# All five instruction queues of a fp32r encoder trunk in an order given by a table, in place of the scheduler's order with hand exceptions

## The chip, the cores and the metric

One core of a Trainium2 chip runs the whole program. Its engines work side by side, each through its own queue of instructions in a fixed order: PE (matmuls; PEld is its weight load), ACT, DVE, POOL, and SP, which here only starts transfers. An instruction waits on semaphores for what others have to deliver, and all behind it on its queue wait too. The metric is the device time of one execution in microseconds (us).

## What is computed

A trunk of two encoder layers over 512 tokens of width 1024, all in float32. Layer 0 mixes tokens by neighbourhood attention on a grid 64 wide (16 heads of 64), layer 1 by multi-head latent attention (low-rank queries and keys, a rotary part, dense). Each layer:

```python
xn = rmsnorm(x, norm_g[i])
y = mixer(xn)            # na: q,k,v,z = xn@w_in ; (attention * silu(z)) @ w_out
h = x + y                # mla: c_q,c_kv,k_rope,z = xn@w_in ; q, kv from the low ranks
gate = sigmoid(rmsnorm(h, ple_norm[i]) @ ple_w_gate[i])
x = h + gate * (p[i] @ ple_w_proj[i])
...
return rmsnorm(x, final_norm)
```

## The kernel before

Every matrix product is made of three fp32r products: each operand is split into a rounded part "hi" and a rest "lo" (ACT makes hi by a copy, DVE or POOL the rest by a subtraction), and hi·hi + hi·lo + lo·hi are summed in PSUM, in matmuls of 128 x 512. PSUM tiles are named by their use: ps_mm, ps_S (scores), ps_T (transposes), ps_O (outputs).

The stages and their times in the run before:

- Start to 45 us: warm-up matmuls, the per-layer embedding of layer 0 (ple, L673, out to memory as pe), the gates z (z_phase) of layer 0 from the raw x, split xT.
- 45 to 105 us: values_seven (L267). The values x@w_v are made by seven products on quarters in place of eight. Its weights W7 and W5 are sums of two quarters: `load` (L273) loads one quarter through SP's queue, and then POOL's queue starts a transfer that accumulates the other into it (L276). W7's tile is later summed with raw pieces on DVE to serve products 6 and 4. `made` splits a piece into whi (ACT) and wlo (DVE). Products 1, 2, 7, 6, 5, 4, 3 follow on PE (L301), between them queries and keys of the first two head pairs (L413). after1, after7, after6 and after5 copy sums out of PSUM (s1, s17, s6) and add them to other banks, so that a product continues a bank which ACT and DVE have just read. All that ACT and DVE do here is written in the order in which it is issued: both are wrapped in InOrder, which adds a dependency of each instruction on the one before.
- 105 to 230 us: the heads of neighbourhood attention (na_head, L536): scores on PE (L558, L559), bias and maximum on DVE, exponential on ACT, scaling on POOL (L582), transposes on PE (L594, L596), split, output (L608). Projections of the next heads (L123) run in between, and POOL starts the accumulating transfers of the gate's weight sums (L730).
- 230 to 395 us: output projection, gate of layer 0 (gate_seven, also in seven products), the low-rank projections of layer 1, z.
- 395 to 560 us: the dense heads (mla_heads, L942). `score` (L1041), `turn` (L1058) and `output` (L1066) are put by hand into 70 steps: at step i the score of step i, the transposes of step i - 3, and outputs two heads back; the projections of the next pair are cut up and added to the steps by `pieces`. qe and qo get their rotary rows by transfers from rh and rl (L117).
- 560 us to the end: output projection, gate of layer 1, final norm, written out by halves of rows.

Order before: the program is traced once; a scheduler with a time model then gives every queue its order by the dependences between tiles. Where that was not wanted, an issue_after written in the code adds an order dependency: 25 places, some on a chain of instructions (PE's in values_seven, na_heads and mla_heads, ACT's and DVE's in values_seven), others on a single one (a load that has to come behind a certain copy, `gn` behind the last load). SP's transfers go through eight semaphores in turn, so that one waits until that of eight earlier has landed.

Of the kernel before, what the change touches and what calls it, by code (L numbers as in the profile page):

```python
# [40 lines left out]
class InOrder:  # L41
# [4 lines left out]
    def __getattr__(self, name):  # L46
        call = getattr(self.engine, name)

        def run(*args, **kw):
            with self.tc.issue_after(self.last.ins) if self.last is not None else nullcontext():  # L50
                self.last = call(*args, **kw)
            return self.last

        return run


class Trunk:
# [122 lines left out]
    def z_phase(self, wap, xT, js, after=None, R=None, ws=None, first=None):  # L180
# [5 lines left out]
        def finish(j, ps):  # L186
            z = zs[j] = self.zp.tile([P, S], F32, name="z", tag="z")
            with self.tc.issue_after(after) if after is not None else nullcontext():
                if R is None:
                    nc.scalar.activation(z, ps, AF.Silu)  # L190
                else:
                    nc.vector.tensor_tensor(out=z, in0=ps, in1=R, op=ALU.mult)
                    nc.scalar.activation(z, z, AF.Silu)
# [73 lines left out]
    def values_seven(self, pool, xT, xk, Q, pair, more):  # L267
# [23 lines left out]
        def product(p):  # L291
# [3 lines left out]
            for c, i in [(0, 0), (0, 1), (1, 0), (1, 1)] if p in (1, 2, 7) else [(0, 0), (1, 0), (0, 1), (1, 1)]:  # L295
# [3 lines left out]
                for j, (l, r) in enumerate(m):  # L299
                    with self.tc.issue_after(self.last_mm.ins):  # L300
                        self.last_mm = nc.tensor.matmul(ps, l, r, start=c == 0 and j == 0 and p in banks,  # L301
                                                        stop=c == 1 and j == 5 and p in (2, 3, 4),
                                                        skip_group_check=True)
# [102 lines left out]
    def na_heads(self, pool, xT, zs, Q, xk, weights, more):  # L406
# [3 lines left out]
        def product(out, w):  # L410
            for i, (l, r) in enumerate(self.terms(w, xT, range(KD))):
                with self.tc.issue_after(self.last_mm.ins):
                    self.last_mm = nc.tensor.matmul(out, l, r, start=i == 0, stop=i == 3 * KD - 1)  # L413
# [13 lines left out]
        def edges(q, last):  # L427
            s0 = []
            for s in q:
                e0 = pool.tile([P, P], F32R, name="s0", tag="s0", bufs=4)  # L430
                with self.tc.issue_after(last.ins):
                    self.act.activation(e0.rearrange("p (a b) -> p a b", a=2),
                                        win(s, 0, P, 0, [[448, 2], [1, 64]]).bitcast(F32), AF.Copy)
# [59 lines left out]
        def attend(j, also):  # L493
            sq, s0, dk, kl = A.pop(j)
            O = []
            for e in range(2):
# [3 lines left out]
                with self.tc.issue_after(self.last_norm.ins):  # L500
                    also(e)
# [34 lines left out]
    def na_head(self, pool, h, sq, s0, dk, kl, vh):  # L536
# [9 lines left out]
        for half in range(2):  # L546
# [25 lines left out]
            for i in range(2):  # L572
                qt = 2 * half + i
                e = ex[:, ecol(qt)]
                with self.tc.issue_after(self.hold):
                    self.last_exp = nc.scalar.activation(e, e, AF.Exp, scale=-1.0, bias=mx[:, qt:qt + 1],  # L576
                                                         accum_out=sm[:, qt:qt + 1])
# [44 lines left out]
    def out_proj(self, wap, oT, res, after, last_mm):  # L622
        nc = self.nc
        for n in range(2):
            ws = [self.load_w(wap[n, c], 1024, extra=n == 1 or c == 3, rest=nc.vector if self.wxn > 5 and c % 2 else None)
                  for c in range(4)]
            for u, t in enumerate(range(NT)):
# [4 lines left out]
                with self.tc.issue_after(last_mm):  # L632
# [842 lines left out]
```

## Time and profile before

| | us |
|---|---|
| median of 3 runs | 652.93 (652.9 to 653.29) |
| profiled execution | 653.56 |
| its span | 651.5 |
| busy: PE, PEld, DVE, ACT, POOL | 640.2, 541.9, 427.7, 453.4, 408.4 |

The span runs from the first to the last instruction that the trace has; about 2 us of the execution lie outside. Matmul ends are modelled, and matmuls overlap, so a time on PE is best counted from start to start. In rows of the trace the first number is the start, the second the time that the group covers; in brackets stands how long the engine was idle before it and what ended that.

### The profile page before, as it was taken

To read this page: it belongs to the slowest core of one execution; us is meant where nothing else is said; L and a number is where in the kernel's file an instruction comes from. 1 tells how busy PE (TensorE), PEld (TensorE's weight loads), DVE (VectorE), ACT (ScalarE), POOL (GpSimd) and SP (SyncE) were. 2 spreads that over 40 slices of the span, in tenths; PEclk is the share of its full clock that TensorE was granted. 3 is DMA by queue.
4 is the path that set the end of the run, shared out by engine and by line. 5 is a ranking of instruction groups with operands and counts; after the bars stand their busy time and mean duration, and the time that the engine had idled before them with its cause. 6 is when DMAs were issued, how large, how long until landed. Compare 5 with 4: busy or idle time off the path is not lost.

```text
span 651.5 us, 9980 instructions
## 1 busy us (share of the span) xinstructions
PE 640.2 (98%) x3299; PEld 541.9 (83%) x3299; DVE 427.7 (66%) x886; ACT 453.4 (70%) x903; POOL 408.4 (63%) x371
## 2 busy tenths in 40 slices
PE   9999999999999999999999999999999999999994
PEld 6888878888888888888999887888888888888884
DVE  6197987565665616569715514898988885474665
ACT  7575766887886733788644535897989897547855
POOL 0471006877978853797655516786969887437974
PEclk9999999999999999999999999999999999999997
DMA  9939725778958989446643245120112223683524
GB/s 326 355 124 306 217 66 179 263 205 217 229 209 217 239 178 342 147 154 188 224 140 102 78 109 156 32 75 24 49 50 66 65 84 112 229 292 126 193 65 162
DMA packets 46131, 107.41 MB, mean 165 GB/s; under 512 B 4736, under 2 KB 17792, under 8 KB 46080
## 3 DMA queue, kind: packets, MB, share of 16 engines
q1 hardware_dynamic: 34608, 87.12, 39.3%
q0 software_dynamic: 11040, 18.88, 13.6%
q10 hardware_dynamic: 432, 0.79, 0.3%
q8 instruction: 26, 0.43, 0.3%
q14 instruction: 25, 0.20, 0.1%
HBM read 95.23 MB, written 25.17 MB: 185 GB/s over the span
## 4 chain that ended last, share of the span: by engine, by line
PE 83%; POOL 1%; ACT 1%; DVE 0%; DMA 0%; issue 0%; POOLq 0%
PE ps_mm L123 27%; PE ps_S L123 10%; PE ps_mm L959 7%; PE ps_T L155 6%; PE ps_T L851 5%; PE ps_O L1071 5%; PE ps_mm L851 3%; PE ps_S L851 3%; PE ps_O L608 2%; PE ps_T L123 2%; PE ps_O L123 2%; PE ps_mm L909 2%; PE ps_T L301 2%; PE ps_T L596 2%; PE ps_S L909 1%; PE ps_S L559 1%
## 5 line engine op out<-in xcount | busy, mean ns | idle before, releaser
L101 POOL TENSOR_TENSOR wwlo<-wraw,wwhi 128x1024 fp32r<-128x1024 f32 (+5 forms) x68 | 122.3, 1810 | 93.5 <-ACT wwhi L100 41.9
L796 POOL TENSOR_TENSOR wlo<-wraw,whi 128x512 fp32r<-128x512 f32 x56 | 72.7, 1331 | 22.3 <-ACT whi L794 20.2
L1056 POOL TENSOR_TENSOR ex<-ex,rc 128x512 f32<-128x512 f32 x64 | 66.2, 1043 | 26.6 <-DVE rc L1055 22.5
L100 ACT ACTIVATE wwhi<-wraw 128x1024 fp32r<-128x1024 f32 (+5 forms) x71 | 55.1, 799 | 34.3 <-PE ps_mm L123 18.9
L1054 ACT ACTIVATE ex<-ps_S,mx 128x512 f32<-128x512 f32 x64 | 44.0, 687 | 12.6 <-DVE mx L1052 10.9
L1052 DVE TENSOR_REDUCE mx<-ps_S 128x1 f32<-128x512 f32 x64 | 43.7, 683 | 8.4 <-PE ps_S L123 7.7
L582 POOL TENSOR_TENSOR ex<-ex,rc 128x128 f32<-128x128 f32 (+1 forms) x64 | 37.5, 701 | 17.7 <-DVE rc L578 17.5
L112 DVE TENSOR_TENSOR pt_lo<-ps_T,pt_hi 128x512 fp32r<-128x512 f32 x64 | 43.1, 680 | 7.1 <-ACT pt_hi L110 6.7
L110 ACT ACTIVATE pt_hi<-ps_T 128x512 fp32r<-128x512 f32 x64 | 37.7, 594 | 3.4 <-PE ps_T L155 3.0
L155 PE MATMUL ps_T<-ident,ex 128*128 128x128 f32 x256 | 38.3, 272 | 0.0
L155 PEld LDWEIGHTS ps_T<-ident,ex 128*128 128x128 f32 x256 | 31.5, 140 | 7.5
L123 PE MATMUL ps_mm<-xh,wwhi 128*128 128x512 f32 x120 | 33.7, 404 | 0.0
L221 DVE TENSOR_TENSOR u<-ps_O,u 64x512 f32<-64x512 f32 x32 | 21.9, 685 | 17.7 <-ACT u L220 17.2
L576 ACT ACTIVATE ex<-ex,mx 128x128 f32<-128x128 f32 (+1 forms) x64 | 30.2, 473 | 4.2 <-DVE mx L565 4.1
L123 PE MATMUL ps_mm<-xl,wwhi 128*128 128x512 f32 x120 | 31.9, 395 | 0.0
L794 ACT ACTIVATE whi<-wraw 128x1024 fp32r<-128x1024 f32 x28 | 29.3, 1057 | 3.2 <-DMA wraw<-sum 2.4
L123 PE MATMUL ps_mm<-xh,wwlo 128*128 128x512 f32 x120 | 31.1, 394 | 0.0
L123 PE MATMUL ps_S<-ke,qe 96*128 96x512 f32 x96 | 28.9, 407 | 0.3 <-DMA qe<-rl 0.3
L123 PE MATMUL ps_S<-ko,qo 128*128 128x512 f32 x96 | 28.9, 409 | 0.0
L959 PE MATMUL ps_mm<-cT,wwhi 128*128 128x512 f32 x94 | 27.7, 393 | 0.0
L220 ACT ACTIVATE u<-ps_O 64x512 f32<-64x512 f32 x32 | 18.9, 591 | 12.0 <-PE ps_O L608 8.8
L225 POOL TENSOR_TENSOR u<-u,z 128x512 f32<-128x512 f32 x16 | 22.6, 1412 | 7.5 <-DVE u L221 7.5
(488 smaller groups left out, 1915.1 us busy)
## 6 DMA issues: line engine op xcount, KB each, us to landing
sum<-gate POOLq DMA_DIRECT2D x12, 1024.0 KB, 8.2
wraw<-na_qk SPq DMA_DIRECT2D x16, 512.0 KB, 4.9
wraw<-sum SPq DMA_DIRECT2D x16, 512.0 KB, 3.3
pe<-pe SPq DMA_DIRECT2D x31, 256.0 KB, 5.9
wraw<-gate SPq DMA_DIRECT2D x12, 512.0 KB, 3.3
wraw<-na_v SPq DMA_DIRECT2D x10, 512.0 KB, 3.4
sum<-sum POOLq DMA_DIRECT2D x4, 1024.0 KB, 11.1
wraw<-na_o SPq DMA_DIRECT2D x8, 512.0 KB, 4.8
```

The source lines that it names most:

```text
L100: nc.scalar.activation(hi[:, c], raw[:, c], AF.Copy)
L101: f = lambda e, c=c: e.tensor_tensor(out=lo[:, c], in0=raw[:, c], in1=hi[:, c].bitcast(F32), op=ALU.subtract)
L110: self.last_copy = self.act.activation(hi, src, AF.Copy, scale=scale)
L112: self.dve.tensor_tensor(out=lo, in0=src, in1=hi.bitcast(F32), op=ALU.subtract)
L123: last = self.last_mm = nc.tensor.matmul(out, l, r, start=i == 0, stop=i == n - 1)
L155: self.last_mm = self.nc.tensor.transpose(t[:, i * P:(i + 1) * P], b, self.ident)
L796: nc.gpsimd.tensor_tensor(out=lo[:, o], in0=raw[:, o], in1=hi[:, o].bitcast(F32), op=ALU.subtract)
L851: mm = nc.tensor.matmul(ps, l, r, start=j == 0 and p in banks, stop=j == 11 and p in (2, 3, 4), skip_group_check=True)
L959: self.last_mm = nc.tensor.matmul(PS[key], *terms[i], start=i == 0, stop=i == len(terms) - 1)
L1052: nc.vector.reduce_max(mx, sp, axis=AX.X, negate=True)
L1054: nc.scalar.activation(ex, sp, AF.Exp, bias=mx, accum_out=sm)
L1056: nc.gpsimd.tensor_tensor(out=ex, in0=ex, in1=rc.to_broadcast([P, S]), op=ALU.mult)
```

## The change

All issue_after's go, and with them the order written into InOrder. In their place a table, ORDER, has for each engine a list of runs of indices: its instructions, numbered as the program writes them, in the order in which they are now to stand. A function, called when the whole trunk is traced, adds an order dependency (no semaphore) of each instruction on the one ahead of it:

```python
ORDER = dict(
    PE=(
        "0-9 11 14-15 12 35 13 16 36 41 37 23-24 42 20 25-26 53-56 21-22 17-19 10 47 43 38 29-30 44 31-33 63-64 57 "
...
def in_order(tc):
    engines = dict(PE="PE", ACT="Activation", DVE="DVE", POOL="Pool", SP="SP")
    traced = [i for i in tc.nc.cur_bb.bb.instructions if "Boundary" not in type(i).__name__]
    behind = mybir.DependencyInfo(mybir.DependencyClass.NoSync, mybir.DependencyReason.DATA)
    for e, runs in ORDER.items():
        mine = [i for i in traced if i.engine == getattr(mybir.EngineType, engines[e])]
        order = []
        for run in runs.split():
            a, _, b = run.partition("-")
            order += mine[int(a):int(b or a) + 1]
        assert len(order) == len(mine) == len(set(i.name for i in order))
        for x, y in zip(order, order[1:]):
            tc.add_manual_dep(y, x.name, behind, reason="in_order")


def trunk_kernel(tc, a):
    with ExitStack() as ctx:
        Trunk(tc, ctx, a).run()
        in_order(tc)
```

The exceptions are taken out in this manner:

```diff
-            with self.tc.issue_after(self.last.ins) if self.last is not None else nullcontext():
-                self.last = call(*args, **kw)
+            self.last = call(*args, **kw)
...
-                    with self.tc.issue_after(self.last_mm.ins):
-                        self.last_mm = nc.tensor.matmul(ps, l, r, start=c == 0 and j == 0 and p in banks,
-                                                        stop=c == 1 and j == 5 and p in (2, 3, 4),
-                                                        skip_group_check=True)
+                    self.last_mm = nc.tensor.matmul(ps, l, r, start=c == 0 and j == 0 and p in banks,
+                                                    stop=c == 1 and j == 5 and p in (2, 3, 4),
+                                                    skip_group_check=True)
```

The instructions, their operands and their number are the same in both programs. The order differs all along: rows that stood together on PE are dealt out among others almost everywhere. Three places follow; the line numbers of the new program are a little smaller.

SP's queue where the weights of values_seven are loaded (W7, W5: the summed weights; wraw_637, 717, 719 and on from na_v: raw pieces of values; wraw_647 and 655: weights of the second head pair). Before:

```order
L252 DMA wraw_543<-na_v 128x1024
L275 DMA W7_519<-na_v 128x2x1024
L275 DMA W5_539<-na_v 128x2x1024
L252 DMA wraw_637<-na_v 128x1024
L457 DMA wraw_647<-na_qk 128x1024
L457 DMA wraw_655<-na_qk 128x1024
L252 DMA wraw_717<-na_v 128x1024
L252 DMA wraw_719<-na_v 128x1024
L252 DMA wraw_733<-na_v 128x1024
```

Now:

```order
L250 DMA wraw_543<-na_v 128x1024
L678 DMA pe03_93<-pe_299 128x512
L250 DMA wraw_637<-na_v 128x1024
L273 DMA W7_519<-na_v 128x2x1024
L452 DMA wraw_647<-na_qk 128x1024
L452 DMA wraw_655<-na_qk 128x1024
L250 DMA wraw_717<-na_v 128x1024
L250 DMA wraw_719<-na_v 128x1024
L273 DMA W5_539<-na_v 128x2x1024
L250 DMA wraw_733<-na_v 128x1024
```

W7's load stands behind one raw piece that it stood ahead of, and W5's behind five.

ACT's queue in the same stage, around the products 6 and 5 (whi_799 and 840 are W5's halves, whi_851 and 890 those of the weight of product 4, s17 and s6 the copies out of PSUM). Before:

```order
L51 ACTIVATE whi_799<-W5_539 128x1024
L51 ACTIVATE da_830<-ps_mm_738 64x512 x2
L51 ACTIVATE db_831<-ps_mm_738 64x512 x2
L51 ACTIVATE s0_836<-sa_787 128x128
L51 ACTIVATE s0_838<-sb_788 128x128
L51 ACTIVATE whi_840<-W5_539 128x1024
L51 ACTIVATE s17_846<-ps_T_804 128x512
L51 ACTIVATE s17_849<-ps_T_805 128x512
L51 ACTIVATE whi_851<-W7_519 128x1024
L51 ACTIVATE s6_884<-ps_T_858 128x512
L51 ACTIVATE s6_887<-ps_O_859 128x512
```

Now:

```order
L50 ACTIVATE whi_851<-W7_519 128x1024
L50 ACTIVATE sa_787<-ps_mm_737 64x512
L50 ACTIVATE sb_788<-ps_mm_737 64x512
L50 ACTIVATE whi_799<-W5_539 128x1024
L50 ACTIVATE whi_840<-W5_539 128x1024
L50 ACTIVATE da_830<-ps_mm_738 64x512 x2
L50 ACTIVATE s17_849<-ps_T_805 128x512
L50 ACTIVATE s17_846<-ps_T_804 128x512
L50 ACTIVATE db_831<-ps_mm_738 64x512
L50 ACTIVATE s6_884<-ps_T_858 128x512
L50 ACTIVATE s6_887<-ps_O_859 128x512
```

whi_851 stands ahead of both halves of W5, and both of these ahead of the copies.

PE's queue at the end of a dense head's transposes (ps_T_5731 is the last of the head whose output is ps_O_5795; ps_S are scores of the next, ps_mm_5747 its projection). Before:

```order
L155 MATMUL ps_T_5731<-ident_71,ex_5628 128x128 x4
L123 MATMUL ps_S_5738<-ke00_3473,qe00_3469 128x512
L123 MATMUL ps_S_5738<-ke01_3474,qe00_3469 128x512
L123 MATMUL ps_S_5738<-ke00_3473,qe01_3470 128x512
L959 MATMUL ps_mm_5747<-cT0_3467,wwhi_5406 128x512 x2
L959 MATMUL ps_mm_5747<-cT1_3468,wwhi_5406 128x512 x2
L155 MATMUL ps_T_5754<-ident_71,ex_5665 128x128 x4
L123 MATMUL ps_S_5764<-ko00_3475,qo00_3471 128x512
L123 MATMUL ps_S_5764<-ko01_3476,qo00_3471 128x512
L123 MATMUL ps_S_5764<-ko00_3475,qo01_3472 128x512
L959 MATMUL ps_mm_5747<-cT0_3467,wwlo_5407 128x512 x2
L155 MATMUL ps_T_5788<-ident_71,ex_5688 128x128 x4
```

Now:

```order
L154 MATMUL ps_T_5731<-ident_71,ex_5628 128x128 x3
L122 MATMUL ps_S_5738<-ke00_3473,qe01_3470 128x512
L154 MATMUL ps_T_5731<-ident_71,ex_5628 128x128
L122 MATMUL ps_S_5764<-ko00_3475,qo00_3471 128x512
L122 MATMUL ps_S_5764<-ko01_3476,qo00_3471 128x512
L122 MATMUL ps_S_5764<-ko00_3475,qo01_3472 128x512
L154 MATMUL ps_T_5754<-ident_71,ex_5665 128x128 x2
L1050 MATMUL ps_O_5795<-pt_hi_5648,vt_5149 128x512 x2
L154 MATMUL ps_T_5754<-ident_71,ex_5665 128x128 x2
L154 MATMUL ps_T_5788<-ident_71,ex_5688 128x128 x2
```

The output's first matmuls, which came behind two more sets of transposes and their scores, now follow after three score matmuls and two transposes.

More of the change, by code (lines that the diff above doesn't have):

```diff
@@ L187, in finish @@
             z = zs[j] = self.zp.tile([P, S], F32, name="z", tag="z")
[L188 to L193, printed above, removed]
+            if R is None:
+                nc.scalar.activation(z, ps, AF.Silu)
+            else:
+                nc.vector.tensor_tensor(out=z, in0=ps, in1=R, op=ALU.mult)
+                nc.scalar.activation(z, z, AF.Silu)
         if ws:
@@ L671, in ple @@
                         for i in (0, 1, 2, 6, 7, 8, 3, 4, 5, 9, 10, 11):
[L672 to L673 removed]
+                            last = nc.tensor.matmul(first[i // 6][0], *first[i // 6][1][i % 6], start=i % 6 == 0, stop=i % 6 == 5)
                 else:
@@ L907, in mla_c @@
                 for j, (l, r) in enumerate(m):
-                    with self.tc.issue_after(self.turned[t + 1].ins) if (part, j) == (0, 12) and t < 3 else nullcontext():
-                        mm = nc.tensor.matmul(ps[:, :wn], l, r, start=j == 0, stop=j == 23)
+                    mm = nc.tensor.matmul(ps[:, :wn], l, r, start=j == 0, stop=j == 23)
                 nc.scalar.activation(cs[t][:, w0:w0 + wn], ps[:, :wn], AF.Copy)
@@ L1145, in mla_heads @@
         rope(0, 0, 9)
[L1146 to L1147 removed]
+        late[0]()
         queries(0, 0, 9, "S")
@@ L1377, in run @@
                     last = self.mla_heads(hpool, x1T, cT, sets, oT)
+ORDER = dict(
+    PE=(
[100 rows of a table added]
+    ),
+    ACT=(
[26 rows of a table added]
+    ),
+    DVE=(
[28 rows of a table added]
+    ),
+    POOL=(
[12 rows of a table added]
+    ),
+    SP=(
[8 rows of a table added]
+    ),
+)
+def in_order(tc):
[11 more added lines that the diff above has]
+            tc.add_manual_dep(y, x.name, behind, reason="in_order")
 def trunk_kernel(tc, a):
```

65 lines of the change are left out of this document (21 added, 44 removed), and 173 rows, old and new, of tables (ACT, DVE, PE, POOL).

## The prediction

> **What bounds the kernel now.** I read the busy time by stage first, then the engine that is busiest there, then what makes it wait. By stage (columns: length, busy time and count of each engine, TensorE clock, DMA share, GB/s):
>
> ```profile
> core 0: us, PE busy (x) PEld busy (x) DVE busy (x) ACT busy (x) POOL busy (x), PEclk, DMA share, GB/s
> 0.00:5.26 5.26, 4.50 (x11) 1.46 (x11) 0.60 (x2) 2.43 (x3) 0.19 (x4) 1.00 0.67 209
> 45.00:105.00 60.00, 58.82 (x264) 48.66 (x263) 52.47 (x68) 35.54 (x51) 9.09 (x8) 1.00 0.60 186
> 105.00:230.00 125.00, 124.67 (x718) 108.41 (x716) 76.35 (x263) 100.39 (x247) 101.15 (x107) 1.00 0.85 223
> 230.00:395.00 165.00, 165.00 (x843) 142.75 (x842) 85.01 (x168) 93.65 (x168) 97.67 (x81) 1.00 0.53 168
> 395.00:560.00 165.00, 164.70 (x894) 138.28 (x893) 131.74 (x259) 137.78 (x298) 126.36 (x117) 1.00 0.22 68
> 642.80:651.50 8.70, 0.00 (x0) 0.00 (x0) 3.79 (x11) 3.06 (x8) 1.54 (x2) 0.61 0.56 210
> ```
>
> From 5.26 us, where the first real matmul starts, to 642.8, PE is busy all but 1.18 + 0.33 + 0.30 = 1.8 us, at full clock. The rest is a start of 5.26 and a tail of 8.70 without matmuls. The change keeps every matmul, so an order alone can win only these gaps, what hides in the modelled ends of matmuls, and some of start and tail. The waits of PE's weight loads name the gaps (total, times, longest):
>
> ```profile
> PEld ps_T L301 <- ACT s L51: 1.4, 1, 1.4
> PEld ps_S L123 <- DMA qe<-rl: 0.7, 1, 0.7
> PEld ps_mm L673 <- ACT whi L652: 0.6, 1, 0.6
> PEld ps_T L596 <- POOL ex L582: 0.5, 1, 0.5
> PEld ps_mm L673 <- DVE wlo L653: 0.3, 1, 0.3
> PEld ps_T L155 <- DVE x1l L112: 0.2, 1, 0.2
> ```
>
> The first, second and fourth are 2.6 by this view and 1.8 by PE's idle time; I take 2.3. The third, fifth and sixth are 1.1; the two at L673 are at the start. So everything there is to win is about 3.5 us, 0.5%. A measurement of this kernel can tell about 0.2%, 1.3 us, from no change; most of the gaps must close, with nothing new, to pass that.
>
> **The change part by part.** *The wait at L301, 88.85 to 90.31 (gain 1.3).* Product 5 of the values needs bank ps_T cleared by ACT's copy s6. ACT in that time:
>
> ```profile
> 87.63 1.20 ACT L51 ACTIVATE s<-ps_T 128x512 f32<-128x512 f32 x2 [2.49 <-DVE ps_T L51]
> 88.72 1.05 ACT L51 ACTIVATE whi<-W 128x1024 fp32r<-128x1024 f32 x1
> 89.67 0.59 ACT L51 ACTIVATE s<-ps_T 128x512 f32<-128x512 f32 x1
> ```
>
> s6 (0.59) stood behind whi_851 (1.05), and that behind two s17 copies that waited 2.49 for DVE. Now whi_851 stands eight rows ahead of s6, and the products it follows on PE are spread through the queries' matmuls. The old cause goes; what is late next is W5 itself, below. I take 1.3 as won.
>
> *The waits at 220 and 401 (gain 0.5 + 0.5).* The first comes from the last neighbourhood head, whose four POOL scalings are slow and collide with DVE; the second from a transfer that started late:
>
> ```profile
> 218.30 3.10 POOL L582 TENSOR_TENSOR ex<-ex,rc 128x128 f32<-128x128 f32 x4 [1.75 <-DVE rc L578]
> 400.08 0.51 SPq L117 DMA_DIRECT2D qe<-rl  x1
> 402.07 0.50 PE L123 MATMUL ps_S<-ke,qe 96*128 96x512 f32 x1 [0.30 <-DMA qe<-rl]
> ```
>
> How far a consumer stands behind its producer on PE I count in matmuls, by this row of the chain: twelve 128x512 in 2.72, so 0.227 each.
>
> ```profile
> 93.36 2.72 PE ps_O L301 x12
> ```
>
> The shortest distance from a neighbourhood head's last score to its first transpose was 2.8 us and is now 4.5; from transpose to output it was 1.7 and is 2.4. At 401 the third score matmul, which needs qe's rest, now has nine more 128x512 matmuls ahead of it: 9 x 0.227 = 2.0 against a wait of 0.7. Both waits go; together 1.0, and what hides the old latencies is those matmuls.
>
> *The start (gain 0.3).* The first real matmul still needs the same two loads and two copies, so 5.26 stays. ple's matmuls (L673) are now mixed with those of the z phase, which are ready at the same time, so of their 0.9 some goes; but the z loads are later in SP's queue, and the third z weight's split is due within about 0.3 us of its use. Bounds -0.9 to +1; I take -0.3.
>
> *The tail (cost 0.3).* After the last matmul the chain is DVE's mean, a POOL power, a half-row scale on DVE, a write:
>
> ```profile
> 642.17 0.75 DVE L1356 SCALAR_TENSOR_TENSOR r<-r,rs,gn 128x512 f32<-128x512 f32 x1
> 645.52 0.99 POOL L1355 TENSOR_TENSOR rs<-mn,half 128x1 f32<-128x1 f32 x1 [0.37 <-DVE mn L1341]
> 646.54 0.75 DVE L1356 SCALAR_TENSOR_TENSOR r<-r,rs,gn 128x512 f32<-128x512 f32 x1 [0.44 <-POOL rs L1355]
> ```
>
> The scale of another row group, r_6162, that ran at 642.17 is now DVE's very last, behind the one at 646.54. DVE then ends 0.75 later, less about 0.4 won in the steps before (the last group's adds stand earlier): +0.3; bounds -0.3 and +0.75.
>
> *W7 and W5, 45 to 90 us (cost 0.2, wide).* These weights are a load by SP and an accumulating transfer by POOL (the last row is a DVE step of the usual size):
>
> ```profile
> 46.89 0.90 SPq L275 DMA_DIRECT2D W<-na_v  x2
> 54.04 1.44 POOL L276 DMA_DIRECT2D W<-na_v  x1 [5.30 <-DMA W<-na_v]
> 56.56 1.22 POOL L276 DMA_DIRECT2D W<-na_v  x1 [1.08 <-DMA W<-na_v]
> 62.59 14.81 SPq L252 DMA_DIRECT2D wraw<-na_v  x5
> 97.97 0.69 DVE L51 TENSOR_TENSOR ps_O<-ps_O,s 128x512 f32<-128x512 f32 x1
> ```
>
> and the DMA view of 45 to 75 us has, with what POOL's other transfers of this size (from gate) take on the page behind it:
>
> ```profile
> q1 hardware_dynamic: 1432, 5.34, 46.7%
> q0 software_dynamic: 544, 2.10, 36.8%
> W<-na_v SPq DMA_DIRECT2D x2, 1024.0 KB, 7.9
> W<-na_v POOLq DMA_DIRECT2D x2, 1024.0 KB, 14.5
> ```
>
> ```profile
> sum<-gate POOLq DMA_DIRECT2D x12, 1024.0 KB, 8.2
> ```
>
> On SP the load of W7 is moved past one piece (wraw_637) and that of W5 past five: wraw_637, 647, 655, 717 and 719. The last two wait for DVE and ACT to free their slots; they went at 62.59 and a few us later, which I put at 65 for both now, as ACT and DVE have their work of that time in nearly the same places. So W5's load goes at 65 instead of 47.3. W7 leaves at about 49.3, lands 6 to 7 later at 56, and its accumulation, no longer sharing with W5's, takes 8 to 12: 64 to 68. Its first use on PE moves ahead, from 77.1 to about 70; from its landing to product 6 at 73.8 lie whi (1.05), three DVE steps (0.69), the sum with raw 717 (two such halves, about 1.2), another whi and some 0.4 of hand-overs, 5.8 in all, so it is due at 68.0. That fits, barely. W5 lands 5 to 7.9 after 65, and its accumulation takes between 8.2 (the gate row) and 14.5 (the row above, two at once): it is there between 78.5 and 88. The software queue's 36.8% of 30 us for two is 5.5 us each at 16 engines, so alone, beside a few raw pieces, I take it near the lower end, at 10: 65 + 6 + 0.3 + 10 = 81.3. ACT must start whi_799 by 83.1 to have s6 done by 88.8: 1.05 + 1.05 and six copies of 0.59 lie between. Cost 0 to 88 - 83.1 = 4.9; I take 0.2 for both. The piece for whi_851, which now stands ahead of whi_799, has to land by 79.3 and leaves at about 73: the same margin.
>
> *The dense heads, 400 to 560 us (cost 0.7).* PE works on score, turn and output there, with queries and keys between. From the last of a head's transposes to the first use of its pt_hi there were at least 3.3 us; now seven of sixteen places have under 2.3, and the shortest (ps_T_5731 to ps_O_5795) has 1.0. ACT's split between them and what may be ahead of it on ACT take:
>
> ```profile
> L110 ACT ACTIVATE pt_hi<-ps_T 128x512 fp32r<-128x512 f32 x64 | 37.7, 594 | 3.4 <-PE ps_T L155 3.0
> L1054 ACT ACTIVATE ex<-ps_S,mx 128x512 f32<-128x512 f32 x64 | 44.0, 687 | 12.6 <-DVE mx L1052 10.9
> ```
>
> So 0.6 fits in 1.0, but not with an exponential of 0.69 just begun. Between none and seven times 0.69, 0 to 4.8, I take 0.1 at each, 0.7: nearer to nothing, as all but the shortest leave room for one of each.
>
> *Sum.* Against the profiled execution, 653.56 (span 651.5 and 2.06 around it): -1.3 - 1.0 - 0.3 + 0.3 + 0.2 + 0.7 = -1.4, so 652.16. That execution was 0.63 above the median of the runs, 652.93; the same difference from the median is **651.5**. Its own range is 650.5 to 652.5.
>
> **The rivals.** *All waits go and none comes, 650.3 (15%).* Then -2.3 - 0.3 alone: 652.93 - 2.6. For it: only six waits are seen in 640 us. Against it: the same slack that closes these is taken elsewhere.
>
> *W5 late, 653 to 656.4 (22%).* A slower ending from one place: its accumulation landing after 83.1 holds ACT, in order, and with it s6 and product 5; each us later is a us of PE. At the far end 651.5 + 4.9 = 656.4. For it: both accumulations were slow before (a median of 14.5), and SP's wait for slots now stands ahead of the load. Against it: with W7's it shared the queue, and PE has other products to do. A PE gap of that length would be the first over 1.4 us, and in all rows above the granted clock is 1.00, through gaps of 1.4. The Trainium skill (TensorE: Matmul & The Clock Gate, HAM oscillation) says that a gap over about 3.4 us halves the clock for as long; no run here shows such a gap inside the work, and by it the far end would be an estimated 1.7 us later still.
>
> *Collisions of DVE and POOL, 653.4 (18%).* What one costs is seen at 98.6 to 102, where two DVE steps (0.69 each elsewhere) lie beside one of POOL:
>
> ```profile
> 98.56 3.48 DVE L51 TENSOR_TENSOR wlo<-wraw,whi 128x512 fp32r<-128x512 f32 x2
> 98.58 2.91 POOL L101 TENSOR_TENSOR wwlo<-wraw,wwhi 128x1024 fp32r<-128x1024 f32 x1 [40.80 <-PE ps_T L301]
> ```
>
> The pair takes 3.48 for 1.37, 2.1 more. The Trainium skill (SBUF — State Buffer, SBUF: two separate sides) calls it an exclusive lock on a shared port pair for DVE steps with two SBUF inputs, held for the whole instruction; the trace agrees, as DVE is done where POOL is. Now the same DVE steps stand ahead of lb1_513, the eighth of eight in a row, which frees the bank for PE's next projection (L123) about 5.4 us after the row's first can start; they take 8 x 0.66 = 5.3. If POOL's step meets them, PE waits 2.1 - 0.1 = 2.0 at 100 us: 651.5 + 1.9 = 653.4. Against it: ACT now feeds POOL later there, so that POOL starts about when DVE ends. That decides by some tenths.
>
> That the table would not take hold is no rival: the changed order of each engine stands in its program.
>
> **How the numbers follow.** Forecast 45%, the three rivals 15, 22 and 18. Faster by over 0.2% is below 651.6: half of the forecast's range and a little more (25), the first rival (15), a share of collisions that cost nothing (2): 42. Slower is above 654.2: W5 late by more than 3 (15), collisions in more than one place (7), waits in the heads near their upper bound (3): 25. Between them 33. The range leaves out a tenth at each end: 650.0, just past the first rival, to 655.5, within the W5 case.
>
> **What would show it.** Right: no PE wait over 0.3 at L301, L596 or at qe<-rl; DVE's last step later than 0.4 us after POOL's last power has been used; PE's waits in 400 to 560 summing to 0.5 to 1.5. Wrong: W5's accumulation landing after 83 with a PE wait on whi or s at L301; a wait of L123 on DVE lb near 100; waits on pt_hi of several us; or the gaps simply gone, and the span below 649.

## The result: 671.26 us, slower by 2.8%

| | before | after |
|---|---|---|
| median of 4 runs, us | 652.91 (652.89 to 653.29) | 671.26 (668.89 to 674.48) |
| profiled execution | 653.56 | 669.96 |
| its span | 651.5 | 667.9 |

The ratio is 1.0283, with a 95% interval of 1.0235 to 1.033. The prediction, 651.5 in a range of 650.0 to 655.5, was wrong, on the other side of no change.

The busy time by stage of the changed kernel, in the columns of the prediction's first rows (length, then busy time and count of PE, PEld, DVE, ACT, POOL, then clock, DMA share, GB/s):

```profile
0.00:5.26 5.26, 4.50 (x11) 1.39 (x11) 0.62 (x2) 2.43 (x3) 0.19 (x4) 1.00 0.64 178
45.00:105.00 60.00, 58.31 (x258) 47.36 (x257) 46.74 (x66) 35.94 (x51) 8.77 (x7) 1.00 0.67 203
105.00:230.00 125.00, 124.10 (x692) 104.32 (x690) 77.35 (x264) 98.80 (x243) 90.65 (x98) 1.00 0.70 187
230.00:395.00 165.00, 163.41 (x834) 138.58 (x833) 83.03 (x168) 93.79 (x171) 109.13 (x89) 1.00 0.61 183
395.00:560.00 165.00, 163.71 (x868) 134.58 (x867) 123.06 (x249) 132.20 (x287) 119.25 (x112) 1.00 0.23 67
```

The start is the same to 5.26, and the clock is full. PE looks as busy as before, 98% of a span that is longer. But read the counts: 692 matmuls in 105 to 230 where there were 718, 868 in 395 to 560 where there were 894. The busy time is a poor witness here, since the modelled end of a matmul covers a short gap behind it: in the four rows from 45 to 560 us PE's idle time grew only from 1.8 to 5.5 us. Counts and starts are not modelled.

So I measured PE's lag. All 3299 matmuls, set end to end at the pitch that each width usually has (from start to start 0.2275 us at 512 columns, 0.1195 at 256, 0.1085 at 128), take about 635 us in either order. The lag of a matmul is its start less the place that it would have in that row. By place in the row (another choice of pitches moves these rows by up to 1 us, and the difference of the two by some tenths):

| at | 5 | 45 | 95 | 150 | 210 | 240 | 300 | 390 | 480 | 540 | 600 |
|---|---|---|---|---|---|---|---|---|---|---|---|
| before | 0.66 | 0.55 | 1.89 | 2.54 | 3.41 | 4.27 | 4.28 | 4.59 | 6.47 | 7.38 | 7.47 |
| after | 1.58 | 2.51 | 5.31 | 7.59 | 11.11 | 11.87 | 14.65 | 16.77 | 19.73 | 22.44 | 23.08 |

The difference at the end, 15.6, is nearly all of the 16.4 between the two profiled executions; the tail gives another 0.7. It grows everywhere and is nowhere given back: 2.0 by 45, 1.5 more by 95, 4.2 more over the heads of layer 0 (95 to 240), 4.6 from there to 390, 3.4 behind it.

There is no large wait to point to. The list of the waits of PE's weight loads (total, times, longest) had six rows before, with one wait in each and 3.7 us in all, beside those at the warm-up. Now it has 41 rows with 57 waits and 23.6 us. Not all of that is lost, since a load starts ahead of its matmul. Among them:

```profile
PEld ps_S L122 <- ACT ex L1033: 1.5, 5, 0.5
PEld ps_S L836 <- ACT X L731: 1.4, 1, 1.4
PEld ps_T L298 <- ACT s L50: 1.3, 1, 1.3
PEld ps_mm L941 <- DVE rh L974: 1.0, 1, 1.0
PEld ps_mm L663 <- ACT whi L643: 0.9, 1, 0.9
PEld ps_S L552 <- DVE Q L50: 0.9, 1, 0.9
PEld ps_S L122 <- DMA qe<-rl: 0.6, 1, 0.6
PEld ps_T L587 <- POOL ex L575: 0.4, 1, 0.4
```

They wait for ACT, DVE, POOL and DMA, in every stage, and none is longer than the longest before. By the chain of work that ended last, PE's own share fell from 83% (there the chain could be followed over 85% of the span) to 72%, and transfers, 0% before, have 9%:

```profile
PE 72%; DMA 9%; DVE 5%; POOL 4%; ACT 3%; issue 3%; SPq 2%; POOLq 0%; DVEq 0%; ACTq 0%
```

Some losses are too short for the list of waits. Here is one, in the timeline of 174 to 178 us. DVE makes pl, PE's output matmul of a head loads it as weights:

```profile
175.59 0.69 DVE L111 TENSOR_TENSOR pl<-ps_T,ph 128x512 fp32r<-128x512 f32 x1
...
176.16 0.30 PE L601 MATMUL ps_O<-ph,Q 128*128 128x256 f32 x1
...
176.33 0.19 PEld L601 LDWEIGHTS ps_O<-pl,Q 128*128 128x128 f32 x1
176.33 0.39 PE L601 MATMUL ps_O<-pl,Q 128*128 128x256 f32 x1
...
176.55 0.39 PE L122 MATMUL ps_mm<-xh,wwhi 128*128 128x512 f32 x1
```

pl is ready at 176.28, the very time at which its matmul was due: 176.16 + 0.12. The weight load starts at 176.33, the matmul with it, and the next matmul only 0.22 later, where 0.12 is usual. No row shows idle time, and 0.15 is gone.

To count such places I took each matmul whose last operand comes after the matmul ahead of it has started (within 0.06), a late arrival, and the lag that was added there. Before there were 6, with 3.1 us of the lag. After there are 82 (41 behind DVE, 30 behind ACT, 8 POOL, 2 DMA, one behind PE), with 15.6: 9 by 45 us, 4 by 100, 23 by 235, 12 by 400, 30 by 580 and 4 behind it. That is 12.5 of the 15.6 difference.

### The profile page after: what moved, and what is told of

Same layout as the page of the kernel before. It is cut to its first block, busy times and chain, and to the rows that moved or that the text cites. A ratio compares the mean times of both kernels' runs of the same rounds, so it can differ in the third digit from the quotient of the medians.

```text
span 667.9 us, 9939 instructions
## 1 busy us (share of the span) xinstructions
PE 651.7 (98%) x3299; PEld 538.4 (81%) x3299; DVE 419.2 (63%) x886; ACT 455.2 (68%) x903; POOL 410.5 (61%) x371
## 4 chain that ended last, share of the span: by engine, by line
PE 72%; DMA 9%; DVE 5%; POOL 4%; ACT 3%; issue 3%; SPq 2%; POOLq 0%; DVEq 0%; ACTq 0%
PE ps_mm L122 24%; PE ps_S L122 10%; PE ps_T L154 5%; PE ps_mm L941 5%; PE ps_O L1050 4%; PE ps_mm L836 3%; PE ps_T L836 3%; DMA W<-na_v 3%; PE ps_O L601 2%; DMA xT<-xT 2%; PE ps_mm L891 2%; PE ps_T L298 2%; DMA wraw<-gate 2%; PE ps_S L836 2%; PE ps_T L589 2%
## 5 line engine op out<-in xcount | busy, mean ns | idle before, releaser
L100 POOL TENSOR_TENSOR wwlo<-wraw,wwhi 128x1024 fp32r<-128x1024 f32 (+5 forms) x68 | 120.1, 1783 | 67.5 <-DVE wlo L50 26.3
L784 POOL TENSOR_TENSOR wlo<-wraw,whi 128x512 fp32r<-128x512 f32 x56 | 74.6, 1359 | 23.1 <-ACT whi L782 20.6
L575 POOL TENSOR_TENSOR ex<-ex,rc 128x256 f32<-128x256 f32 (+1 forms) x64 | 37.5, 644 | 29.8 <-DVE rc L571 24.1
L1031 DVE TENSOR_REDUCE mx<-ps_S 128x1 f32<-128x512 f32 x64 | 43.6, 684 | 10.6 <-PE ps_S L122 10.0
L122 PE MATMUL ps_mm<-xh,wwhi 128*128 128x512 f32 x120 | 37.0, 406 | 0.0
L122 PE MATMUL ps_mm<-xh,wwlo 128*128 128x512 f32 x120 | 36.9, 401 | 0.0
L122 PE MATMUL ps_mm<-xl,wwhi 128*128 128x512 f32 x120 | 35.5, 397 | 0.0
L122 PE MATMUL ps_S<-ke,qe 96*128 96x512 f32 x96 | 32.8, 413 | 0.4 <-DMA qe<-rl 0.3
L122 PE MATMUL ps_S<-ko,qo 128*128 128x512 f32 x96 | 30.9, 408 | 0.3 <-DMA qo<-rl 0.3
L111 DVE TENSOR_TENSOR pl<-ps_T,ph 128x384 fp32r<-128x384 f32 (+1 forms) x32 | 19.8, 622 | 17.1 <-ACT ph L109 16.7
L836 PE MATMUL ps_T<-whi,X 128*128 128x512 f32 x96 | 28.2, 394 | 0.5 <-DVE X L732 0.5
```

Source lines behind the costliest of these rows:

```text
L100: f = lambda e, c=c: e.tensor_tensor(out=lo[:, c], in0=raw[:, c], in1=hi[:, c].bitcast(F32), op=ALU.subtract)
L111: self.dve.tensor_tensor(out=lo, in0=src, in1=hi.bitcast(F32), op=ALU.subtract)
L122: last = self.last_mm = nc.tensor.matmul(out, l, r, start=i == 0, stop=i == n - 1)
L575: self.last_norm = nc.gpsimd.tensor_tensor(out=e, in0=e, in1=rc[:, qt:qt + 1].to_broadcast([P, e.shape[1]]), op=ALU.mult)
L784: nc.gpsimd.tensor_tensor(out=lo[:, o], in0=raw[:, o], in1=hi[:, o].bitcast(F32), op=ALU.subtract)
L836: mm = nc.tensor.matmul(ps, l, r, start=j == 0 and p in banks, stop=j == 11 and p in (2, 3, 4), skip_group_check=True)
```

## The experiments

Three theories stood at the outset. *One*: results arrive too late all along, because the new order uses them close behind their making. *Two*: dealing out matmuls of many kinds costs PE itself. *Three*: the loss comes down from a few late transfers (W7 and W5, the gate's weights).

**The table alone (e1).** The new program's code, with the old order written in its table:

```diff
     PE=(
-        "0-9 11 14-15 12 35 13 16 36 41 37 23-24 42 20 25-26 ...
+        "0-17 23-24 29-30 18-22 35 41 47 53 25-28 31-34 36-38 42 ...
```

> The new program's code with the table holding the old program's order on all five queues. All theories: 652.9, as before, within 0.5. Another time would mean that the table itself, and not the order in it, costs.

It took 652.84 (652.32 to 653.87), ratio 0.9995 (0.9984 to 1.0006). What was lost lies in the order, not in how it is stated.

**PE alone (e2, e3).** Only the matmuls, with their widths and banks in the order of before (e2) and after (e3), on operands that are never changed; no other engine has work:

```diff
-        Trunk(tc, ctx, a).run()
-        in_order(tc)
+    for run in SEQ.split():
+        k, o = run[0], banks[int(run[1])]
...
+                mm = nc.tensor.matmul(o[:, :wide[k]], w[r, l], w[r, :wide[k]], start=True, stop=True)
```

> Leaves out everything but the 3299 matmuls and transposes, in the old order on PE, with the same widths and PSUM banks, on operands that lie ready; the output is not the trunk's. Theory 1 (late arrivals: PE's waits for ACT and DVE end too late for the weight load to hide): 635 of matmuls and some 15 around them, 645 to 652. It is the partner of the next run; only the difference counts.

> The same with the new order on PE. Theory 1: within 0.5 us of its partner, as the order alone costs PE nothing. Theory 2 (the fine mixing of products costs PE time at every switch): longer by 10 to 16 us.

642.38 (641.19 to 642.77) and 643.16 (642.47 to 643.9). The busy line of each page, e2:

```profile
PE 639.0 (100%) x3299; PEld 542.0 (85%) x3299; DVE 1.9 (0%) x3; ACT 1.9 (0%) x2; POOL 0.2 (0%) x4
```

and e3:

```profile
PE 639.1 (100%) x3299; PEld 540.5 (84%) x3299; DVE 1.8 (0%) x3; ACT 1.9 (0%) x2; POOL 0.2 (0%) x4
```

The difference of the medians, 0.8, lies within the spread of either, and in the traces the last matmuls start 0.1 apart. Theory two falls: to PE by itself these two orders are the same. Both came below what had been expected of the old order; some 10 us of the old order's time are its tail and its waits.

**Stage by stage (e4, e5, e6, e9).** Each is the old order with the new one in one stage, on all five queues: up to 46 us (e4), 100 to 240 (e5), 229 to 402 (e6), from 395 on (e9). The edit is in the table alone; in e4, PE's queue begins with the numbers of the new one and goes on with those of the old:

```diff
     PE=(
-        "0-17 23-24 29-30 18-22 35 41 47 53 25-28 31-34 36-38 42 39-40 ...
+        "0-9 11 14-15 12 35 13 16 36 41 37 23-24 42 20 25-26 53-56 ...
...
         "1797-1802 1863-1895 1803-1808 1896-1927 1809-1814 1928-1997 ...
```

> New order on all queues up to 46 us of its trace, old order from there. Theory 1 (losses of the stages add up): the 1.9 us that PE lies behind there stay, 654.8, range 654.3 to 655.3. Theory 3 (late transfers, W5's above all, set the loss and the rest follows): 653 to 653.5. Theory 2: 653 to 654, by the share of the mixed matmuls.

e4: 654.83, ratio 1.0025 (1.0013 to 1.0037), 1.8 more than before.

> Old order up to 100 us, new order for what is left of the new program's first 240 us (the neighbourhood heads), old order from there. Theory 1: 3.5 to 4.5 us on top, 656.4 to 657.4, from PE's lag in the trace between 100 and 240 us. Theory 3: 653 to 654, as the late loads of W7 and W5 lie ahead of it. Theory 2: 656 to 658 as well.

e5: 668.1, ratio 1.0222 (1.0201 to 1.0242), far from what was expected, but for a reason of its own. Over the heads its lag grew 4.2 more than before, as expected. Then, at the seam where the new order ends and the old begins, one wait stands in the list:

```profile
PEld ps_mm L122 <- POOL ol L227: 7.8, 1, 7.8
```

The old rest puts the output projection first, whose operand the new order of POOL had made later. That is no loss of either kernel. I use e5 for the 4.2 only.

> Old order up to 229 us, new order up to 402 us of the new trace (output projection, gate of layer 0, low ranks), old order from there. Theory 1: 3.7 on top, 656.0 to 657.2. Theory 3: 653.5 to 655, one late gate weight alone. Theory 2: 653 to 654, since this stage is mixed least.

e6: 657.33, ratio 1.0066 (1.0041 to 1.0091), 4.0 more, a little over what was expected. About 0.8 of it lies at the seam behind its stage, where the old rest waits longer for qe<-rl (1.0 instead of 0.7). The transfers that make the gate's summed weights, the last two of which the changed kernel starts late (e11 below), still start at their old times in e6, the last at 226.

> Old order up to 395 us, new order from there to the end (dense heads, gate of layer 1, tail). Theory 1: PE's lag in the new trace grows by 4.5 from there to the end and the tail by 0.7: 658.1, range 657 to 659, a wait at the seam aside. Theory 3 (late transfers of the first half): 653 to 654.

e9: 657.49, ratio 1.0064 (1.005 to 1.0078), 4.3 more; 30 of its late arrivals lie between 400 and 580, as many as in the changed kernel.

So every stage costs its own part: 1.8, 4.2, 4.0 and 4.3, and with the 1.5 that the lag shows between 45 and 95, which was not run alone, 15.8 against 16.4 between the profiled executions. That it fits so well is partly luck, as e6 has 0.8 from its seam and lacks what the late sums cost. The loss does not come down from one early transfer: e6 and e9 pay theirs behind an undisturbed beginning.

**W5 earlier (e8).** The changed kernel, with one row moved on SP's queue:

```diff
 L273 DMA W_519<-na_v 128x2x1024
+L273 DMA W_539<-na_v 128x2x1024
 L452 DMA wraw<-na_qk 128x1024 x2
 L250 DMA wraw<-na_v 128x1024 x2
-L273 DMA W_539<-na_v 128x2x1024
```

> The new program with one row of SP's queue moved: W5's load directly behind W7's, past four raw pieces, about 15 us earlier. Theory 1: 1.1 less, the one wait at L301: 669 to 671. Theory 3: 4 us less or more, 664 to 667.

671.42, ratio to before 1.028 (1.0249 to 1.0311): nothing won, less than either theory had expected. In the changed kernel W5's load left at 68.1, and its accumulation was issued at 75.9 and took 10.3 (the view of line 274):

```profile
DMA to landing us min/median/max: 9.9/10.1/10.3
```

so W5 was whole at 86.2. In e8 it was issued at 61.6 and took 15.6, so whole at 77.2, 9 us earlier. Yet the wait for which it was to be the cause stayed:

```profile
PEld ps_T L298 <- ACT s L50: 1.2, 1, 1.2
```

So W5 is not what this wait hangs on, and theory three falls for W5. It does not fall for the other transfers of this place. In e8 two raw pieces that were loaded beside W5's accumulation landed at 73.9 and 77.1, where in the changed kernel they landed at 70.7 and 72.6, and DVE's sum had to wait for one (timeline of e8):

```profile
73.97 1.23 DVE L50 TENSOR_TENSOR W<-W,wraw 128x1024 f32<-128x1024 f32 x1 [1.05 <-DMA wraw<-na_v]
```

Between places 70 and 80, PE's lag grew 2.6 there instead of 0.8. And in the changed kernel the chain of work that leads to the wait at L298 comes from W7, the other summed weight:

```profile
51.60 7.54 DMA W<-na_v
59.47 9.92 DMA W<-na_v
69.41 1.07 ACT whi L50
```

From there it goes through DVE's sums to whi_851, s6 and PE at 93.14. No run has W7 earlier, so what its lateness costs is not shown.

**Room on PE alone (e7).** The changed kernel, in which 90 matmuls of the first 400 us that come too soon after their operand are moved up to five places back; for instance, with two projections now ahead of a score:

```diff
+L409 MATMUL ps_mm<-xh_158,whi 128x512
 L552 MATMUL ps_S<-da,s_666 128x256
-L409 MATMUL ps_mm<-xh_158,whi 128x512
+L409 MATMUL ps_mm<-xh_159,whi 128x512
```

> The new program with only PE's order changed, up to 400 us: 90 matmuls whose operands arrived later than 0.6 us ahead in the trace stand up to five places later, behind others that were ready. Theory 1: a third to two thirds of the 11 us lost there come back, 664 to 667.5. Theory 2: 670 to 673, as the mixing is finer still. Theory 3: 669 to 673.

667.6 (665.38 to 671.72), ratio to before 1.022 (1.0168 to 1.0272), 3.7 less than the changed kernel by the medians, though the intervals overlap, and 1.1 less by the profiled executions (668.86): the time alone does not show a gain. The trace shows one over the heads. There the late arrivals went from 23 to 10 and their cost from 3.6 to 1.2; the lag grew 3.9 instead of 6.6. Part of it was lost again where a transfer is late whatever PE's order is: between 240 and 270 the lag grew 4.6 instead of 1.9, with this wait for the gate's operand (1.4 in the changed kernel):

```profile
PEld ps_S L836 <- ACT X L731: 2.8, 1, 2.8
```

**The sums' transfers (e11).** In the changed kernel the last two accumulating transfers of the gate's weights leave at 271 and 280 us, where before they left at 222 and 226 (timeline of POOL):

```profile
271.25 1.31 POOL L720 DMA_DIRECT2D sum<-sum  x1
280.28 1.29 POOL L720 DMA_DIRECT2D sum<-gate  x1
```

There they run beside the loads of the gate's raw weights; from 262 to 288 the DMA view has

```profile
q1 hardware_dynamic: 2011, 6.27, 67.3%
q0 software_dynamic: 1375, 1.39, 34.6%
...
wraw<-gate SPq DMA_DIRECT2D x3, 512.0 KB, 7.7
```

where a load of that size took 3.3 in the same stretch before. ACT waits for one of these loads, and ACT's copy X, for which PE waits at L836, stands behind it in the queue:

```profile
281.72 1.06 ACT L782 ACTIVATE whi<-wraw 128x1024 fp32r<-128x1024 f32 x1 [1.66 <-DMA wraw<-gate]
```

e11 puts all sixteen transfers that make these sums (half of them add, half only copy) on POOL's queue back behind the instruction that they followed in the old order, in the midst of the heads' scalings:

```diff
-L575 TENSOR_TENSOR ex<-ex,rc 128x256 x3
+L575 TENSOR_TENSOR ex<-ex,rc 128x256
+L720 DMA sum_101<-gate 1024x256
+L575 TENSOR_TENSOR ex<-ex,rc 128x256 x2
...
-L720 DMA sum_101<-gate 1024x256
-L720 DMA sum_99<-gate 1024x256
+L720 DMA sum_100<-gate 1024x256
```

> The new program with POOL's sixteen accumulating transfers of the gate's weight sums (L720) put back behind the POOL instruction that they followed in the old order, the last two at about 225 in place of 271 and 280 us. Theory 1 alone (slack on the engines): 670 to 672.5, PE's lag between 255 and 300 us grows by 1.9 as before. With the transfers as a part of it (theory 3 for this stage): that growth falls under 0.8, 668.5 to 670.

672.81 (672.3 to 673.3), ratio to before 1.0298 (1.0284 to 1.0312), a little over theory one's range. Between 240 and 300 the lag now grew 1.2 instead of 2.8, so the late sums did cost something there, by these two executions about 1.6: theory three is right for this part of the gate stage. But over the heads it grew 10.7 instead of 6.6, behind POOL:

```profile
PEld ps_T L587 <- POOL ex L575: 4.3, 3, 1.7
```

Each transfer instruction holds POOL for 0.8 to 1.8, and the scalings behind it are used at once in this order. What the one place won, the next, having no room, lost.

**The price of a late result (e10).** The disputed cost by itself, on a kernel that computes nothing of the reference: a matmul, ACT's copy of its result, a number of matmuls that need nothing, then a matmul that loads the copy as weights; 30 times for each number from 8 down to 1.

```diff
+                mm(o, w[:, :P], w)
+                put("ACT", nc.scalar.activation(t, o, AF.Copy))
+                for k in range(between):
+                    mm(banks[4 + k % 2], w[:, k % 4 * P:(k % 4 + 1) * P], w)
+                mm(banks[6], t[:, :P], w)
```

> Leaves out the trunk: on PE a matmul, ACT's copy of its result, some matmuls on ready operands, and a matmul whose weights are that copy; 30 times each with 8, 7, 6, 5, 4, 3, 2 and 1 of them between. By the rows of the trace the copy is there about 1.1 us after the first matmul's start. Theory 1 (the weight load has to start with the matmul ahead): 5 between and more cost nothing, 4 cost 0.2 to 0.35 each, 3 cost 0.45 to 0.6, 2 cost 0.65 to 0.85. If only a result later than the consuming matmul's own start cost: 4 nothing, 3 0.2, 2 0.4.

| matmuls between | 8 to 5 | 4 | 3 | 2 | 1 |
|---|---|---|---|---|---|
| lost each time, us | 0 | 0.113 | 0.343 | 0.567 | 0.796 |

The copy is there 1.14 to 1.16 us after the first matmul's start, which is five pitches of 0.23. With four matmuls between, the consumer is due at just that time and starts 0.007 late, but the one behind it comes 0.11 late. From there each matmul less costs a whole pitch. So the loss is what the result is late, and 0.11 on top; it is nothing if the result is there one matmul earlier than its consumer is due. The measured prices lie between the two that were expected. The timeline with three between:

```profile
300.22 0.60 ACT L64 ACTIVATE t<-b 128x512 fp32r<-128x512 f32 x1 [0.88 <-PE b L56]
300.87 0.19 PEld L56 LDWEIGHTS b<-w,t 128*128 128x128 f32 x1 [0.49 <-ACT t L64]
300.88 0.50 PE L56 MATMUL b<-w,t 128*128 128x512 f32 x1
300.98 0.89 PEld L56 LDWEIGHTS b<-w 128*128 128x128 f32 x4
301.22 1.09 PE L56 MATMUL b<-w 128*128 128x512 f32 x4
```

The load of t waits for ACT, its matmul starts 0.01 behind it and has 0.50 where 0.39 is usual, and the next starts 0.34 later instead of 0.23. The Trainium skill (TensorE: Matmul & The Clock Gate, Step-by-step: what each phase is for) says that a weight load is taken ahead of matmuls in flight, so that the next weights are loaded while a matmul runs. That agrees with the loads here that wait for nothing. I read the 0.11 as the part of a waiting load that stands in the open because it could not be taken ahead; the rows fit that, and no run tests it by itself.

The changed kernel shows the same. Of its 82 late arrivals, 15 came within 0.05 of the time at which they were due, and cost 0.15 each; 11 that were 0.05 to 0.15 late cost 0.17, six of 0.15 to 0.3 cost 0.39, eight later ones, 0.65 late on average, 0.74. The forty that were early by more than 0.05 cost 0.05 each. In the eighty that a wait on an engine ends, 7.7 us are lateness and 6.9 are on top of it.

**The old order with four rows moved (e12).** What this change might have won is seen where its slack is not taken. e12 has the old order and this alone:

```diff
 DVE
-L50 TENSOR_TENSOR wlo<-W_539,whi 128x512 x4
 L50 TENSOR_TENSOR ps_T<-ps_T,s_635 128x512
 L50 TENSOR_TENSOR ps_T<-ps_T,s_642 128x512
+L50 TENSOR_TENSOR wlo<-W_539,whi 128x512 x4
 PE
-L589 MATMUL ps_T<-ident,ex 128x128
 L601 MATMUL ps_O<-pl,Q_680 128x192
 L601 MATMUL ps_O<-ph,Q_503 128x192
 L601 MATMUL ps_O<-pl,Q_503 128x192
 L601 MATMUL ps_O<-ph,Q_680 128x256
-L589 MATMUL ps_T<-ident,ex 128x128 x4
+L589 MATMUL ps_T<-ident,ex 128x128 x5
...
-L122 MATMUL ps_S<-ke_3473,qe_3470 128x512
 L941 MATMUL ps_mm<-cT_3467,wwhi 128x512 x3
 L941 MATMUL ps_mm<-cT_3468,wwhi 128x512
+L122 MATMUL ps_S<-ke_3473,qe_3470 128x512
```

> The old order by table with its three longest waits taken away by hand: on DVE the two additions of s1 to ps_T stand ahead of the four wlo steps of W5, on PE one transpose of the last neighbourhood head stands four places later and one score matmul of qe's rest four later. Theory 1 (a wait removed where there is slack stays removed, as stages add up): 1.3 + 0.5 + 0.5 less, 650.6, range 650.2 to 651.5. If the gain is eaten by later waits: 652 to 653.

651.04 (650.74 to 652.42) against 653.18 of the kernel before on the same chip: ratio 0.9969 (0.9957 to 0.998), 0.3% below the kernel before and clear of its noise. The waits of PE's weight loads that are left outside the warm-up:

```profile
PEld ps_mm L663 <- ACT whi L643: 0.5, 1, 0.5
PEld ps_mm L663 <- DVE wlo L644: 0.4, 1, 0.4
PEld ps_S L122 <- ACT ex L1033: 0.2, 1, 0.2
```

and from 45 to 105 us and from 105 to 230 its PE has no gap at all:

```profile
45.00:105.00 60.00, 60.00 (x270) 49.83 (x269) 52.23 (x68) 36.70 (x53) 9.22 (x9) 1.00 0.64 198
105.00:230.00 125.00, 125.00 (x719) 108.72 (x718) 77.54 (x265) 100.25 (x248) 102.47 (x108) 1.00 0.85 220
```

## Why the prediction was wrong

**The bound was right.** PE's matmuls set the time, everything there was to win was some 3 us, and the order by itself costs PE nothing that shows (e2, e3). The three gaps that the prediction put at 2.3 are worth that where only they are closed: e12 won 2.1.

**The step that failed is the dense heads, "seven of sixteen places", "0.1 at each, 0.7".** Its mechanism was right, results used too soon after their making. Two things in it were not. The count was taken in one stage, from one kind of step, while the slack was gone in the whole program: 82 late arrivals, 30 of them in that stage, where they cost 4.1 instead of 0.7. And the price was taken as the time that a result is late, so that a distance that just fits was free; e10 and the 15 arrivals that came on time show 0.11 to 0.15 for each of those. The upper bound, seven times 0.69, 4.8, would have held for that stage. The larger part of the loss stands where the sum has no such term at all: the neighbourhood heads, 4.2 by e5, and the stage of the gate, 4.0 by e6 and 4.6 by the lag, in which the late start of the sums' transfers, also without a term, has about 1.6. The sign that the prediction gave for being right in the dense heads even came: PE's own idle time from 400 to 560 is 1.2, within its 0.5 to 1.5, since the modelled ends hide the rest.

**The wait at L301 (forecast -1.3): it stayed, 1.3 by the view of the weight loads, 1.4 before.** "The old cause goes" was right; the new one was in the order shown, and the prediction priced it as a margin. ACT from 81 us in the changed kernel:

```profile
81.68 1.06 ACT L50 ACTIVATE whi<-W 128x1024 fp32r<-128x1024 f32 x1 [3.47 <-DVE W L50]
85.36 1.06 ACT L50 ACTIVATE whi<-W 128x1024 fp32r<-128x1024 f32 x1 [2.62 <-DVE W L50]
...
87.53 2.01 ACT L50 ACTIVATE whi<-W 128x1024 fp32r<-128x1024 f32 x2
...
92.49 0.60 ACT L50 ACTIVATE s<-ps_T 128x512 f32<-128x512 f32 x1
```

The row at 85.36 is whi_851. W5's halves (87.53) and all the copies stood behind it, s6 came at 92.49, and PE had its product 5 at 93.14 instead of going on at 92.1. whi_851 waited for DVE's sum with a raw piece. The prediction took that piece for the worry, due by 79.3; it left at 73.9 and was there at 78.2. It was DVE that was late; its first and last steps of that row:

```profile
77.30 1.29 DVE L50 TENSOR_TENSOR Q<-ps_S,Q 128x512 fp32r<-128x512 f32 x2 [1.67 <-ACT Q L50]
...
84.02 1.23 DVE L50 TENSOR_TENSOR W<-W,wraw 128x1024 f32<-128x1024 f32 x1
```

From 77.30 to 85.25 DVE has ten steps without a pause, and the sum is the last; the prediction did not add them up. By the chain of work shown under e8 this row hangs in turn on W7, which the prediction had due at 68.0 ("That fits, barely") and which came at 69.4. In e8 the same row ends at 86.55, 1.3 later, with W5 there and a raw piece late, and the same wait follows.

**The waits at 220 and 401 (forecast -1.0): both went, and others of their kind came elsewhere.** The 0.4 at L587 is at 149.9 us; PE waits for qo<-rl at 422.97 (0.28 of its own idle time) and for qe<-rl at 527.0:

```profile
527.00 0.50 PE L122 MATMUL ps_S<-ke,qe 96*128 96x512 f32 x1 [0.32 <-DMA qe<-rl]
```

The steps looked at the places that had been tight, not at the others of their kind.

**The start (forecast -0.3): +2.0 of lag by 45 us**, beyond the upper bound of 1; e4 has 1.8. The third z weight's split, said to be due "within about 0.3 us" of its use, is among nine late arrivals there, with a wait of 0.3 (whi L1203); the longest are ple's operands (whi L643, 0.9 and 0.8) and a split of xT (rh L1182, 0.6).

**The tail (forecast +0.3): +0.7**, at the upper bound of 0.75. DVE's last two steps stand one behind the other, as foreseen:

```profile
662.66 1.41 DVE L1331 SCALAR_TENSOR_TENSOR r<-r,rs,gn 128x512 f32<-128x512 f32 x2 [0.44 <-POOL rs L1330]
```

the 0.4 that was to be won ahead of them did not come.

**W7 and W5 (forecast +0.2):** W7 was whole at 69.4, past its 64 to 68, as its load left at 51.6 instead of 49.3; W5 at 86.2, within 78.5 to 88 but five behind the value taken, mostly as its load left at 68.1 instead of 65. The lower bound of 8.2 for an accumulation came from a row in which eight of twelve transfers only copy; 9.9 and 10.3 were measured. The stage lost 1.5 more than before by the lag, with the wait at L301 in it. The sign of the rival *W5 late* came, W5 after 83 and a wait on s at L301, but not its mechanism: whi_799 started at 87.53, right behind the copies ahead of it, when W5 had been there for 1.3, and in e8, with W5 there 9 us earlier, the wait stayed. (That rival's words on the clock, 1.00 "in all rows above", leave out the row of the tail, 0.61.)

**Collisions of DVE and POOL** did not come: at the place in question POOL's step started at 103.45, just when DVE's two wlo steps, 1.28 for both, had ended. *All waits go* is not what this change did; e12 did it, at 651.04.

**What stays open.** What W7's lateness costs was not run, and the price of the late sums rests on one execution of each kernel. The sum of the stages is 15.8; the medians differ by 18.3. The profiled execution is one of the faster ones, and four runs of the new order spread over 5.6 us. The four of the old order beside them spread over 0.4, but nineteen others of it, run with e1 to e4, over 3.4, so that much less can be read from the spread than it seems. An order without slack may pass on every change in a transfer's time, which would fit e7's spread of 6.3; but e4, e8, e9 and e11, all with much of that order, spread by 1 to 4. One place is known to vary: PE's wait for the gate's operand is 1.4 in the changed kernel's trace, 2.6 in e8's and 2.8 in e7's. Whether it makes the spread was not traced.

## What to carry to other kernels

Where one engine is 98% busy, an order can win only its few gaps, and it pays for each result that it uses too soon; list them first, and mend each with the one row that causes it (four rows, -2.1 us) before a whole order is replaced (+18). Judge an order by its slack over the whole program: count the matmuls whose operand is ready less than one matmul ahead of its turn, and price each at its lateness plus 0.11 us. Whoever takes a result used just in time for free can spend all the slack there is.

## What the runs showed of the hardware

A weight load whose operand comes just on time costs PE 0.11 us (e10, 128 x 512), and the matmul's row books that as busy time (0.50 instead of 0.39 in the rows under e10), not as a wait. The lag from start to start shows it.

PE took the same 3299 matmuls in both orders, in long runs of one kind or finely mixed, at the same speed: 642.38 and 643.16 us, and 639.0 and 639.1 busy (e2, e3).

e5's seam has the first long gap inside the work, 7.4 us from 244.2 to 251.6, and the granted clock (the number behind POOL's count) fell in it and came back some 3 us after the work went on:

```profile
244.00:248.00 4.00, 0.17 (x1) 0.00 (x0) 0.00 (x0) 0.00 (x0) 0.38 (x1) 1.00 0.42 169
248.00:250.00 2.00, 0.00 (x0) 0.00 (x0) 0.00 (x0) 0.00 (x0) 2.00 (x3) 0.51 0.20 15
252.00:254.00 2.00, 2.00 (x6) 1.52 (x6) 0.00 (x0) 0.00 (x0) 2.00 (x2) 0.50 1.22 194
254.00:256.00 2.00, 2.00 (x13) 1.77 (x12) 0.00 (x0) 0.09 (x1) 1.07 (x1) 0.79 1.24 195
256.00:258.00 2.00, 2.00 (x10) 1.64 (x9) 0.69 (x1) 0.50 (x1) 0.69 (x1) 1.00 1.24 199
```

The seam cost 9.3 us of lag, 7.4 and about 1.9 for the slow matmuls behind it. The Trainium skill (TensorE: Matmul & The Clock Gate, HAM oscillation) has a gap over about 3.4 us halve the clock; this run agrees, and the many short gaps of the changed kernel, at a clock of 1.00, agree from the other side.

An accumulating transfer of 1 MB into a weight took 9.9 and 10.3 us in the changed kernel, where the two were issued 16.4 us apart, and 10.6 and 15.6 in e8, where they were 2.5 apart, as in the kernel before (12.1 and 16.9). Raw pieces of 0.5 MB loaded beside the later one took 8.4 and 9.9 in e8, 4.7 and 4.9 in the changed kernel. An instruction that starts one of the sums' transfers holds POOL for 0.8 to 1.8 us (e11).
